# Small matrix products of two side lanes, written one at a time between large ones

## The chip, the cores and the metric

One core of one Trainium2 chip. The time is the device time of one execution in microseconds, the median of several runs; a profile is of one execution.

## What is computed

A decoder trunk of two layers on one sequence of 512 tokens with 1024 channels, all in float32. Cut to what matters here:

```python
for l in range(DEPTH):                       # 2
    h = rmsnorm(x, attn_norm[l])
    q_a, kv_a, g_a, q_b, k_b, v_b, uv_c = split(h @ w_in[l])
    o_a = nsa_attention(...)                 # 8 heads: compressed, selected and window branches, gated
    o_b = diff_attention(...)                # 4 heads, two softmax maps each, a = p0 - lam * p1
    o_c = chunked_sgu(uv_c, ...)             # per chunk of 128 tokens: lower-triangular product, times u
    gates = sigmoid(h @ w_merge[l] + b_merge[l])
    mixed = sum over branches of gates * (o @ w_branch)
    x = x + mixed @ w_out[l]
    h = rmsnorm(x, ffn_norm[l])
    x = x + (silu(h @ w_ffn1[l]) * (h @ w_ffn3[l])) @ w_ffn2[l]
return rmsnorm(x, final_norm)
```

## The kernel before

**The main stream.** Everything that multiplies by a weight matrix is a list of tasks (`layer_tasks`): the input projections, gates and branches (`merge_tasks`), the output projection, the feed-forward part. Weights come in chunks of 128 x 1024, are split into a high and a low half (ScalarE writes `wh` at L163, VectorE or GpSimd `wl` at L166), and each product of a 128 x 128 block is three matmuls of 512 columns: high x high, low x high, high x low (`mm3`, L184 to L186). `fm` and `tm` are generators around it; after three matmuls they yield 650, their rough length in ns. These 512-column matmuls are called large products here.

**The lanes.** Attention, the gating mixer and the softmax of the compressed branch are not tasks, but generators in two lanes (`aux_tasks`). Their TensorE work is small: transposes of 128 x 128 blocks of softmax weights (`sB` in `nsa`, L936; `sB` in `diff`, L1050), products of 128 columns (`sC` in `diff`, L1061; `prod` in `sgu_aux`, L764; `s0` in `cmp_soft`, L812), and logits of 128 to 512 columns (L878, L879). A lane's yield also states ns.

**What sets the order.** `run` goes through the tasks. Whenever the main stream yields c ns, each lane's balance grows by c (half of it in three slow tasks), and the lane is stepped until its balance is used up. So between two yields of the main stream, three large products, a lane writes all that it has between two of its own yields. `tick` counts main steps (for evacuations that are written so many steps later) and ns. A task that needs a lane's result steps the lanes until it is there. The tile framework then orders each engine's instructions by its own rules, with manual dependencies at a few places.

**Banks.** PSUM tiles come from four tags: three banks g (main stream), two banks s (logits, the mixer), two banks t (transposes and small products) and one bank o. A transposed block is read out of its bank t twice: ScalarE copies the high half (L937), VectorE subtracts for the low half (L945, written in `sL`). For the compressed softmax the same are L851 and L855.

Of the kernel before, what the change touches and what calls it, by code (L numbers as in the profile page):

```python
# [21 lines left out]
P, TT, KT, FT = 128, 4, 8, 22  # L22
# [9 lines left out]
D_MX, D_ACT, D_OA, D_XP = (2, 4), (7, 19), (3, 6, 17), 2  # L32
D_NORM = (10, 13)
W_NSA, W_DIFF, LAG = 470, 1200, 4
WARM = 14
SLOW = ("QA", "KB", "QB")
POOLED = {"g": 512}
# [43 lines left out]
class Kern:  # L81
# [35 lines left out]
        self.timed.append((self.clock + ns, key, fn))  # L117
        self.timed.sort(key=lambda e: e[0])

    def tick(self, ns=0):  # L120
        self.now += 1
        self.clock += ns
        while self.pending and self.pending[0][0] <= self.now:
            self.pending.pop(0)[2]()
        while self.timed and self.timed[0][0] <= self.clock:
            self.timed.pop(0)[2]()
# [52 lines left out]
    def mm3(self, out, w, x, k, kx, first, last, ts=slice(0, S)):  # L179
        nc = self.nc  # L180
        wh, wl = w
        xh, xl = x[kx] if isinstance(x[kx], tuple) else (x[kx][:, 0, :], x[kx][:, 1, :])
        c = slice(k * P, (k + 1) * P)
        nc.tensor.matmul(out, wh[:, c], xh[:, ts], start=first, stop=False)  # L184
        nc.tensor.matmul(out, wl[:, c], xh[:, ts], start=False, stop=False)  # L185
        nc.tensor.matmul(out, wh[:, c], xl[:, ts], start=False, stop=last)  # L186

    def fm(self, i0, evacs, x, K=KT, late=False, hooks=None, tag="g"):

        hooks = hooks or {}  # L190
        n = len(evacs)
        outs = [None] * n
        seq = [(m, k) for m in range(n) for k in range(K)]
        if late:
            cuts = late if isinstance(late, tuple) else (K - 1, K)
            seq = [(m, k) for a, b in zip((0,) + cuts, cuts) for m in range(n) for k in range(a, b)]
        for q, (m, k) in enumerate(seq):
            w = self.chunk(i0 + m)
            if outs[m] is None:
                outs[m] = self.bank(tag)  # L200
            self.mm3(outs[m], w, x, k, k, k == 0, k == K - 1)
            if (late and ((m == 0 and k == 5) or (m and k == K - 1))) or (not late and k == 3):
                self.ahead(i0 + m)
            if q in hooks:
                hooks[q]()
            if k == K - 1:
                evacs[m](outs[m])
            yield 650

    def tm(self, i0, x, evac, cuts, n, cs=None):  # L210

        nc = self.nc
        cs = range(len(cuts) - 1) if cs is None else cs
        if cs[0] == 0:
            self.tm_outs = [self.bank(b) for b in "gggo"]
        outs = self.tm_outs
        for c in cs:
            wh, wl = self.chunk(i0 + c - cs[0])
            for t in range(TT):
                ts = slice(t * P, (t + 1) * P)  # L220
                o = outs[t][:, :n]
                for k in range(cuts[c], cuts[c + 1]):
                    sl = slice((k - cuts[c]) * n, (k - cuts[c] + 1) * n)
                    nc.tensor.matmul(o, x[k][:, 0, ts], wh[:, sl], start=(k == 0), stop=False)  # L224
                    nc.tensor.matmul(o, x[k][:, 0, ts], wl[:, sl], start=False, stop=False)  # L225
                    nc.tensor.matmul(o, x[k][:, 1, ts], wh[:, sl], start=False, stop=(k == KT - 1))  # L226
                    yield 650 * n / 512
                if t == 0:
                    self.ahead(i0 + c - cs[0])
                if k == KT - 1:  # L230
                    evac(t, outs[t])
# [511 lines left out]
    def sgu_aux(self):  # L743
# [17 lines left out]
        def prod(t):  # L761
            ps = self.bank("s", [P, 4, P])
            for g in range(4):
                nc.tensor.matmul(ps[:, g, :], self.V[t][:, g * P:(g + 1) * P], wT[:, g, :],  # L764
                                 start=True, stop=True)
            return ps

        def mix(t, ps):
            tmp = self.t2("stmp", (P, 4, P))
# [17 lines left out]
        for t in range(TT + 2):  # L787
            if t + 1 < TT:
                norm(t + 1)
            if t < TT:  # L790
                pss[t] = prod(t)
                yield 1300
                tmps[t] = mix(t, pss.pop(t))
                yield 1300
            if t - 2 >= 0:
                split(t - 2, tmps.pop(t - 2))
                yield 650
# [3 lines left out]
    def cmp_soft(self, g, part):  # L801
# [5 lines left out]
        def s0():  # L807
            ps = st["ps"] = self.bank("t", [P, 4, P])
            for t in range(TT):
                ts = slice(t * P, (t + 1) * P)  # L810
                for ab in range(2):
                    nc.tensor.matmul(ps[:, t, :], raw[:, ab, ts],  # L812
                                     self.KAB[:, ab, g].rearrange("p h n -> p (h n)"),
                                     start=(ab == 0), stop=(ab == 1))
            st["e"] = e = self.t2("ce", (P, 4, 4, 32))
            st["ef"] = e.rearrange("p t h n -> p t (h n)")
            st["e3"] = e.rearrange("p t h n -> p (t h) n")
            nc.vector.tensor_tensor(st["ef"], ps, self.r4[:, :, None].to_broadcast([P, 4, P]), op=OP.mult)
# [27 lines left out]
        def s4():  # L846
            pt = st["pt"] = self.bank("t")
            for t in range(TT):
                nc.tensor.transpose(pt[:, t * P:(t + 1) * P], st["ef"][:, t, :], self.ident)
            pc = self.PcT[g] = self.t4("pcT", [P, 2, S], F32R)  # L850
            nc.scalar.activation(pc[:, 0, :], pt, AF.Copy)  # L851

# [1 line left out]
            pc = self.PcT[g]  # L854
            nc.vector.tensor_tensor(pc[:, 1, :], st["pt"], pc[:, 0, :].bitcast(F32), op=OP.subtract)  # L855

        for w, f in (((2600 * (g == 0), lambda: None), (1300, s0), (1300, s1), (1300, s2), (2600, ex)), ((2600, s3), (2600, s4), (1300, s5)))[part]:
            f()
            yield w

    def soft(self, s, n, i, sm=None):
# [20 lines left out]
    def nsa(self, g):  # L882
# [39 lines left out]
        def sB(v, part):  # L922
# [11 lines left out]
            for j in js:  # L934
                for h in range(2):
                    nc.tensor.transpose(pt[:, j - 2 * part, h, :], E[2 * v + h][:, j * P:(j + 1) * P], self.ident)  # L936
            nc.scalar.activation(hi, pt[:, 0:len(js)], AF.Copy)  # L937
            LO.append((lo, pt[:, 0:len(js)], hi))
            if js[-1] == i:
# [56 lines left out]
        for u in range(n + b + 3):  # L996
            if u == n:
                self.done.add("rows%d%d" % (g, l))
            if ok(u - 1):
                sN(u - 1)  # L1000
            if ok(u):
                sA(u)
            yield W_NSA
            w = u - b
            sL()
            if w % 2 and ok(w):
                sB(w // 2, 0)
            elif w % 2 == 0 and ok(w - 2):
                sB(w // 2 - 1, 1)
            if w % 2 == 0 and ok(w - 4):  # L1010
                sC(w // 2 - 2)
            yield W_NSA
        self.ensure("oa")


    def diff(self, p):
# [6 lines left out]
        def sA(u, j):  # L1023
            c, i = units[u]
            n = (i + 1) * P
            s = self.logits(q2[c][:, j], kh[c][:, j, :n], kl[c][:, j, :n], i)
            E[u, j] = self.soft(s, (i + 1) * P, i)

        def sN(u):
# [15 lines left out]
        def sB(u):  # L1045
            c, i = units[u]
            e = E.pop(u)
            pt = self.bank("t", [P, 4, P])
            for j in range(i + 1):
                nc.tensor.transpose(pt[:, j, :], e[:, j * P:(j + 1) * P], self.ident)  # L1050
            AT[u] = self.t2("at", (P, 4, P))
            nc.scalar.activation(AT[u][:, 0:i + 1, :], pt[:, 0:i + 1, :], AF.Copy)

        def sC(u):
# [5 lines left out]
            for j in range(i + 1):  # L1060
                nc.tensor.matmul(OB[c][:, i, :], at[:, j, :],  # L1061
                                 self.Vb[j // 2][:, j % 2, hd * P:(hd + 1) * P],
                                 start=(j == 0), stop=(j == i))
            if i == TT - 1:
                fin(c)

# [36 lines left out]
        for u in range(n + 4):  # L1103
            if ok(u - 1):
                sN(u - 1)
            if ok(u):
                sA(u, 0)
            yield W_DIFF
            if ok(u):
                sA(u, 1)  # L1110
            if ok(u - 2):
                sM(u - 2)
            yield W_DIFF
            if ok(u - 3):
                sB(u - 3)
            if ok(u - 4):
                sC(u - 4)
            yield W_DIFF
        if p == 1:
            yield from self.settle("ob", 600)  # L1120

# [94 lines left out]
    def ffn2(self, i0, m, evac):  # L1216
# [3 lines left out]
        for k in range(FT):  # L1220
# [2 lines left out]
            w = self.chunk(i0 + c)  # L1223
            if pos == 2:
                self.ahead(i0 + c)
            self.mm3(ps, w, self.act, pos, k, k == 0, k == FT - 1)
            if k == FT - 1:
                evac(ps)
            yield 650

# [23 lines left out]
    def ffn2_tail(self, i0):  # L1256
# [5 lines left out]
        m = KT - 1  # L1262
        for half in range(2):
            ts = slice(256 * half, 256 * half + 256)
            ps = self.bank("g")[:, :256]
            for k in range(FT):
                c, pos = divmod(m * FT + k, 8)
                w = self.chunk(i0 + c)
                if pos == 2 and half == 0:
                    self.ahead(i0 + c)  # L1270
                self.mm3(ps, w, self.act, pos, k, k == 0, k == FT - 1, ts)
                if k == FT - 1:
                    self.fin_evac(m, ts)(ps)
                if k == 12:
# [217 lines left out]
    def run(self):  # L1492
# [16 lines left out]
        def step(j):  # L1509
# [7 lines left out]
                c[1] = f()  # L1517
            try:
                w = next(c[1])
                self.tick(w if j else 0)  # L1520
                return w
            except StopIteration:
                self.done.add(lanes[j][c[0]][0])
# [5 lines left out]
        for n, chunks, f, need in tasks:  # L1529
# [4 lines left out]
                        raise RuntimeError("blocked: %s needs %s" % (n, x))  # L1534
            pace = (1, 0.5 if n[:2] in SLOW else 1)
            for c in f(i0):
                self.tick(c)
                for j in range(len(lanes)):
                    cur[j][2] += c * pace[j]
                    while cur[j][2] > 0:  # L1540
# [118 lines left out]
```

## Time and profile before

| | before |
|---|---|
| median of 3 runs | 1770.16 us (1769.95 to 1770.19) |
| the profiled execution | 1770.18 us, span 1768.3 us |
| TensorE busy | 1755.5 us, 99% of the span, 8436 matmuls |
| TensorE weight loads | 1465.0 us, 83% |
| VectorE / ScalarE / GpSimd busy | 968.9 / 751.4 / 354.0 us (55% / 42% / 20%) |
| granted TensorE clock | full (0.999) |

The span is the profiled part of the execution. Busy time of TensorE counts modelled ends: matmuls overlap in the records (one lasts 0.39 us and the next starts 0.23 us after it), so the time that a matmul costs is read from start to start. Weight loads are a separate row (PEld) and run beside matmuls.

### The profile page before, as it was taken

To read this page: it belongs to the slowest core of one execution; us is meant where nothing else is said; L and a number is where in the kernel's file an instruction comes from. 1 tells how busy PE (TensorE), PEld (TensorE's weight loads), DVE (VectorE), ACT (ScalarE), POOL (GpSimd) and SP (SyncE) were. 2 spreads that over 40 slices of the span, in tenths; PEclk is the share of its full clock that TensorE was granted. 3 is DMA by queue.
4 is the path that set the end of the run, shared out by engine and by line. 5 is a ranking of instruction groups with operands and counts; after the bars stand their busy time and mean duration, and the time that the engine had idled before them with its cause. 6 is when DMAs were issued, how large, how long until landed. Compare 5 with 4: busy or idle time off the path is not lost.

```text
span 1768.3 us, 22696 instructions
## 1 busy us (share of the span) xinstructions
PE 1755.5 (99%) x8436; PEld 1465.0 (83%) x8436; DVE 968.9 (55%) x1774; ACT 751.4 (42%) x1317; POOL 354.0 (20%) x355
## 2 busy tenths in 40 slices
PE   9999999999999999999999999999999999999998
PEld 7888888888888888888888888888888888888887
DVE  6877665665644444433366786746656444444223
ACT  6557663444333332222244576634533333322222
POOL 0244332444120000000012343214430200000000
PEclk9999999999999999999999999999999999999999
DMA  7571126532322222223344612255413232222221
GB/s 259 190 221 68 54 72 185 173 120 90 113 96 96 96 95 96 96 99 125 109 145 146 220 47 68 80 171 161 149 66 114 95 107 96 96 95 96 100 101 50
DMA packets 67726, 205.78 MB, mean 116 GB/s; under 512 B 8992, under 2 KB 9376, under 8 KB 67616
## 3 DMA queue, kind: packets, MB, share of 16 engines
q1 hardware_dynamic: 67472, 204.29, 34.6%
q8 instruction: 67, 1.10, 0.3%
q14 instruction: 43, 0.35, 0.1%
q10 hardware_dynamic: 144, 0.04, 0.0%
HBM read 185.29 MB, written 19.01 MB: 116 GB/s over the span
## 4 chain that ended last, share of the span: by engine, by line
PE 97%; DVE 1%; ACT 1%; DMA 0%; issue 0%; POOL 0%; SPq 0%; DVEq 0%; ACTq 0%; POOLq 0%
PE ps_g L184 26%; PE ps_g L185 26%; PE ps_g L186 26%; PE ps_o L958 2%; PE ps_t L936 2%; PE ps_s L879 2%; PE ps_g L224 2%; PE ps_s L878 2%; PE ps_g L225 2%; PE ps_g L226 2%; PE ps_o L1061 1%; DVE wl L166 1%; PE ps_o L226 1%; PE ps_o L224 1%; PE ps_o L225 0%; PE ps_t L1050 0%
## 5 line engine op out<-in xcount | busy, mean ns | idle before, releaser
L163 ACT ACTIVATE wh<-wr 128x1024 fp32r<-128x1024 f32 (+2 forms) x320 | 315.4, 989 | 654.2 <-PE ps_g L186 351.7
L184 PE MATMUL ps_g<-xg,wh 128*128 128x512 f32 x1400 | 553.8, 396 | 0.0
L185 PE MATMUL ps_g<-xg,wl 128*128 128x512 f32 x1400 | 546.8, 391 | 0.0
L186 PE MATMUL ps_g<-xg,wh 128*128 128x512 f32 x1400 | 546.2, 390 | 0.1
L166 DVE TENSOR_TENSOR wl<-wr,wh 128x1024 fp32r<-128x1024 f32 (+1 forms) x308 | 367.5, 1195 | 234.8 <-ACT wh L163 231.3
L186 PEld LDWEIGHTS ps_g<-xg,wh 128*128 128x128 f32 x1400 | 262.8, 188 | 56.2 <-DVE xg L283 1.0
L184 PEld LDWEIGHTS ps_g<-xg,wh 128*128 128x128 f32 x1400 | 263.2, 188 | 50.4 <-ACT xg L280 0.5
L185 PEld LDWEIGHTS ps_g<-xg,wl 128*128 128x128 f32 x1400 | 263.3, 188 | 49.0 <-DVE wl L290 0.3
L869 ACT ACTIVATE e<-e,nm 128x384 f32<-128x384 f32 (+2 forms) x192 | 107.2, 559 | 89.0 <-DVE nm L867 85.0
L184 PE MATMUL ps_g<-act,wh 128*128 128x512 f32 (+1 forms) x374 | 141.2, 378 | 0.0
L185 PE MATMUL ps_g<-act,wl 128*128 128x512 f32 (+1 forms) x374 | 140.8, 376 | 0.0
L186 PE MATMUL ps_g<-act,wh 128*128 128x512 f32 (+1 forms) x374 | 140.8, 376 | 0.0
L497 POOL TENSOR_TENSOR acc<-acc,sq 128x512 f32<-128x512 f32 x18 | 29.3, 1626 | 433.6 <-ACT sq L496 433.6
L919 POOL TENSOR_SCALAR e<-e,sm,ga 128x128 f32<-128x128 f32 (+3 forms) x128 | 82.1, 652 | 111.8 <-DVE sm L915 88.7
L867 DVE CUSTOM_DVE_ANT_0 e<-ps_s,con 128x384 f32<-128x384 f32 (+2 forms) x192 | 90.8, 483 | 22.3 <-PE ps_s L879 20.7
L1202 DVE TENSOR_TENSOR fb<-ps_g,R 128x512 f32<-128x512 f32 x44 | 30.4, 691 | 129.1 <-PE ps_g L186 129.1
L166 POOL TENSOR_TENSOR wl<-wr,wh 128x512 fp32r<-128x512 f32 x48 | 72.6, 1513 | 117.7 <-ACT wh L163 117.7
L1193 DVE TENSOR_TENSOR fa<-ps_g,R 128x512 f32<-128x512 f32 x44 | 30.4, 691 | 95.7 <-PE ps_g L186 95.7
L186 PEld LDWEIGHTS ps_g<-act,wh 128*128 128x128 f32 x374 | 70.3, 188 | 13.0
L184 PEld LDWEIGHTS ps_g<-act,wh 128*128 128x128 f32 x374 | 70.3, 188 | 12.9
L185 PEld LDWEIGHTS ps_g<-act,wl 128*128 128x128 f32 x374 | 70.4, 188 | 12.8
L945 DVE TENSOR_TENSOR pt<-ps_t,pt 128x512 fp32r<-128x512 f32 (+1 forms) x96 | 56.7, 597 | 27.4 <-ACT pt L937 27.2
(248 smaller groups left out, 2474.2 us busy)
## 6 DMA issues: line engine op xcount, KB each, us to landing
wr<-in_wst SPq DMA_DIRECT2D x266, 512.0 KB, 3.3
rp_d<-pc SPq DMA_DIRECT2D x112, 128.0 KB, 3.6
wr<-in_wst SPq DMA_DIRECT2D x52, 256.0 KB, 2.6
q<-rp_d SPq DMA_DIRECT2D x16, 512.0 KB, 5.9
kh<-rp_d SPq DMA_DIRECT2D x24, 256.0 KB, 5.8
xT<-in_xT SPq DMA_DIRECT2D x7, 512.0 KB, 6.2
kl<-rp_d SPq DMA_DIRECT2D x12, 256.0 KB, 6.8
xtok<-in_xtok SPq DMA_DIRECT2D x4, 512.0 KB, 8.7
```

Source lines behind the costliest of these rows:

```text
L163: nc.scalar.activation(h[:, :w], t[:, :w], AF.Copy)
L166: eng.tensor_tensor(lo[:, a:b], t[:, a:b], h[:, a:b].bitcast(F32), op=OP.subtract)
L184: nc.tensor.matmul(out, wh[:, c], xh[:, ts], start=first, stop=False)
L185: nc.tensor.matmul(out, wl[:, c], xh[:, ts], start=False, stop=False)
L186: nc.tensor.matmul(out, wh[:, c], xl[:, ts], start=False, stop=last)
L224: nc.tensor.matmul(o, x[k][:, 0, ts], wh[:, sl], start=(k == 0), stop=False)
L225: nc.tensor.matmul(o, x[k][:, 0, ts], wl[:, sl], start=False, stop=False)
L226: nc.tensor.matmul(o, x[k][:, 1, ts], wh[:, sl], start=False, stop=(k == KT - 1))
L867: nc.vector.tensor_tensor_reduce(out=e[:, :n], in0=s[:, :n], in1=self.mask[:, S - n:], scale=-0.125, scalar=3e38, op0=OP.add, op1=OP.min, ...
L869: nc.scalar.activation(e[:, :n], e[:, :n], AF.Exp, bias=nm, scale=-1.0, accum_out=sm)
L919: nc.gpsimd.tensor_scalar(e[:, :n], e[:, :n], sm[:, h:h + 1], self.ga[:, i, b:b + 1], op0=OP.mult, op1=OP.mult)
L945: nc.vector.tensor_tensor(lo, pt, hi.bitcast(F32), op=OP.subtract)
```

## The change

Every matmul of the main stream and most small ones of the lanes get a yield of their own. A yield that is a tuple is a part of a step: it adds ns and lets the lanes run, but does not count as a step for evacuations that are written later. The main stream now yields 650 / 3 ns after each of the three matmuls, and a lane yields the same after each transpose or small product; the lanes' other yields are made shorter, so that a step's sum stays about as it was.

```diff
+BIG = 650 / 3
...
-    def tick(self, ns=0):
-        self.now += 1
+    def tick(self, ns=0, step=1):
+
+        self.now += step
...
         nc.tensor.matmul(out, wh[:, c], xh[:, ts], start=first, stop=False)
+        yield BIG,
         nc.tensor.matmul(out, wl[:, c], xh[:, ts], start=False, stop=False)
+        yield BIG,
         nc.tensor.matmul(out, wh[:, c], xl[:, ts], start=False, stop=last)
...
-            self.mm3(outs[m], w, x, k, k, k == 0, k == K - 1)
+            yield from self.mm3(outs[m], w, x, k, k, k == 0, k == K - 1)
...
-            yield 650
+            yield BIG
...
                 nc.tensor.matmul(ps[:, g, :], self.V[t][:, g * P:(g + 1) * P], wT[:, g, :],
                                  start=True, stop=True)
-            return ps
+                yield BIG,
+            pss[t] = ps
...
-                pss[t] = prod(t)
-                yield 1300
+                yield from prod(t)
+                yield 450
...
-        for w, f in (((2600 * (g == 0), lambda: None), (1300, s0), (1300, s1), (1300, s2), (2600, ex)), ((2600, s3), (2600, s4), (1300, s5)))[part]:
-            f()
+        for w, f in (((2600 * (g == 0), lambda: None), (450, s0), (1300, s1), (1300, s2), (2600, ex)), ((2600, s3), (1750, s4), (1300, s5)))[part]:
+            parts = f()
+            if parts is not None:
+                yield from parts
...
                     nc.tensor.transpose(pt[:, j - 2 * part, h, :], E[2 * v + h][:, j * P:(j + 1) * P], self.ident)
+                    yield BIG,
...
-            yield W_NSA
+            yield W_NSA * 0.6
...
-                sB(w // 2, 0)
+                yield from sB(w // 2, 0)
             elif w % 2 == 0 and ok(w - 2):
-                sB(w // 2 - 1, 1)
+                yield from sB(w // 2 - 1, 1)
...
-            yield W_NSA
+            yield W_NSA / 4
...
                 nc.tensor.transpose(pt[:, j, :], e[:, j * P:(j + 1) * P], self.ident)
+                yield BIG,
...
-            yield W_DIFF
+            yield W_DIFF * 0.75
...
             if ok(u - 3):
-                sB(u - 3)
+                yield from sB(u - 3)
             if ok(u - 4):
-                sC(u - 4)
-            yield W_DIFF
+                yield from sC(u - 4)
+            yield W_DIFF * 0.5
...
                 w = next(c[1])
-                self.tick(w if j else 0)
+                part = isinstance(w, tuple)
+                w = w[0] if part else w
+                self.tick(w if j else 0, not part)
...
             for c in f(i0):
-                self.tick(c)
+                part = isinstance(c, tuple)
+                c = c[0] if part else c
+                self.tick(c, not part)
```

`tm`, `ffn2` and the products of `sC` in `diff` are treated the same way; the last quarter of the last projection (`ffn2_tail`) keeps its steps.

TensorE's queue in layer 0, where the gating mixer starts (`prod`, L764 before and L770 after, into `ps_s`; L184 to L186 before are L186, L188 and L190 after), before:

```order
L764 MATMUL ps_s<-sw,v 128x128 x4
L184 MATMUL ps_g<-xg,wh 128x512
L185 MATMUL ps_g<-xg,wl 128x512
L186 MATMUL ps_g<-xg,wh 128x512
L184 MATMUL ps_g<-xg,wh 128x512
```

and now:

```order
L770 MATMUL ps_s<-sw,v 128x128
L188 MATMUL ps_g<-xg,wl 128x512
L770 MATMUL ps_s<-sw,v 128x128
L190 MATMUL ps_g<-xg,wh 128x512
L770 MATMUL ps_s<-sw,v 128x128
L186 MATMUL ps_g<-xg,wh 128x512
L770 MATMUL ps_s<-sw,v 128x128
L188 MATMUL ps_g<-xg,wl 128x512
```

Four products of one chunk, one clump before, have one large product between each two now.

TensorE's queue in the head of the first attention lane of layer 0 (L936 before and L947 after are transposes into `ps_t`, L878/L879 and L889/L890 logits, L958/L970 and L969/L981 products with the values), before:

```order
L936 MATMUL ps_t<-con,e 128x128 x2
L184 MATMUL ps_g<-oc,wh 128x512
L936 MATMUL ps_t<-con,e 128x128 x4
L185 MATMUL ps_g<-oc,wl 128x512
L186 MATMUL ps_g<-oc,wh 128x512
L936 MATMUL ps_t<-con,e 128x128 x4
L878 MATMUL ps_s<-kh,q_1217 128x384
L879 MATMUL ps_s<-kl,q_1217 128x384
L184 MATMUL ps_g<-xg,wh 128x512
```

and now:

```order
L947 MATMUL ps_t<-con,e 128x128 x8
L889 MATMUL ps_s<-kh,q_1213 128x512
L970 MATMUL ps_o<-pt,v_1129 128x512
L890 MATMUL ps_s<-kl,q_1213 128x512
L889 MATMUL ps_s<-kh,q_1213 128x512
L890 MATMUL ps_s<-kl,q_1213 128x512
L970 MATMUL ps_o<-pt,v_1129 128x512
L970 MATMUL ps_o<-pt,v_1129 128x2x128 x2
L947 MATMUL ps_t<-con,e 128x128 x6
L970 MATMUL ps_o<-pt,v_1129 128x512 x2
L970 MATMUL ps_o<-pt,v_1129 128x2x128 x2
L981 MATMUL ps_o<-pcT,VCS 128x256 x4
```

Here the lane's products have moved together: these 30 products have no large product of the main stream between them. The same stands in layer 1.

## Rows read from the trace of the kernel before

**Rows 1.** The page: busy us of each engine, its share of the span, its instructions.
```profile
PE 1755.5 (99%) x8436; PEld 1465.0 (83%) x8436; DVE 968.9 (55%) x1774; ACT 751.4 (42%) x1317; POOL 354.0 (20%) x355
```

**Rows 2.** Waits of PE: line, what ended it; us, times, longest.
```profile
PE ps_g L224 <- DVE raw L679: 2.5, 2, 1.9
...
PE ps_t L936 <- DVE pcT L855: 0.9, 2, 0.4
PE ps_s L764 <- DVE stmp L770: 0.6, 1, 0.6
```

**Rows 3.** Timeline of PE, large products alone: start us, us, instruction.
```profile
600.08 0.39 PE L186 MATMUL ps_g<-xg,wh 128*128 128x512 f32 x1
...
611.19 0.39 PE L184 MATMUL ps_g<-xg,wh 128*128 128x512 f32 x1
```

**Rows 4.** Timeline of PE around a clump of four transposes.
```profile
441.30 0.60 PE L1090 MATMUL ps_t<-con,do 128*128 128x128 f32 x4
441.66 0.48 PE L184 MATMUL ps_g<-xg,wh 128*128 128x512 f32 x1
441.97 0.40 PE L185 MATMUL ps_g<-xg,wl 128*128 128x512 f32 x1
...
444.51 0.39 PE L184 MATMUL ps_g<-xg,wh 128*128 128x512 f32 x1
```

**Rows 5.** Timeline of PE around a clump of eight fp32 records.
```profile
1245.65 1.05 PE L1061 MATMUL ps_o<-vb,at 128*128 128x128 f32 x8
...
1247.92 0.22 PE L878 MATMUL ps_s<-kh,q 128*128 128x128 f32 x1
```

**Rows 6.** Timeline of PE around a transpose that stands alone.
```profile
332.89 0.28 PE L1050 MATMUL ps_t<-con,e 128*128 128x128 f32 x1
332.92 0.48 PE L184 MATMUL ps_g<-xg,wh 128*128 128x512 f32 x1
333.24 0.40 PE L185 MATMUL ps_g<-xg,wl 128*128 128x512 f32 x1
...
333.70 0.22 PE L878 MATMUL ps_s<-kh,q 128*128 128x128 f32 x1
```

**Rows 7.** Timeline of PE around another lone transpose.
```profile
1206.29 0.27 PE L1050 MATMUL ps_t<-con,e 128*128 128x128 f32 x1
...
1206.63 0.39 PE L185 MATMUL ps_g<-xg,wl 128*128 128x512 f32 x1
```

**Rows 8.** Timeline of PEld, the weight loads around the transpose of rows 6.
```profile
332.66 0.14 PEld L1050 LDWEIGHTS ps_t<-con,e 128*128 128x128 f32 x1
332.89 0.19 PEld L184 LDWEIGHTS ps_g<-xg,wh 128*128 128x128 f32 x1
333.01 0.19 PEld L185 LDWEIGHTS ps_g<-xg,wl 128*128 128x128 f32 x1
```

**Rows 9.** Timelines of PE, ACT and DVE in the head of attention, layer 0.
```profile
143.85 0.58 ACT L851 ACTIVATE pcT<-ps_t 128x512 fp32r<-128x512 f32 x1
144.46 0.69 DVE L855 TENSOR_TENSOR pcT<-ps_t,pcT 128x512 fp32r<-128x512 f32 x1
145.29 0.41 PE L936 MATMUL ps_t<-con,e 128*128 128x128 f32 x2
146.25 0.42 DVE L945 TENSOR_TENSOR pt<-ps_t,pt 128x256 fp32r<-128x256 f32 x1
146.37 0.72 ACT L869 ACTIVATE e<-e,nm 128x512 f32<-128x512 f32 x1 [0.24 <-DVE nm L867]
146.45 0.40 PE L186 MATMUL ps_g<-oc,wh 128*128 128x512 f32 x1
146.82 0.63 PE L936 MATMUL ps_t<-con,e 128*128 128x128 f32 x4
```

**Rows 10.** Timeline of PE, products of 256 columns in a row.
```profile
83.71 0.28 PE L595 MATMUL ps_s<-wl,xh 128*128 128x256 f32 x1
...
84.42 0.28 PE L595 MATMUL ps_s<-wl,xh 128*128 128x256 f32 x1
```

More of the change, by code (lines that the diff above doesn't have):

```diff
@@ L224, in tm @@
                     nc.tensor.matmul(o, x[k][:, 0, ts], wh[:, sl], start=(k == 0), stop=False)
+                    yield BIG * n / 512,
                     nc.tensor.matmul(o, x[k][:, 0, ts], wl[:, sl], start=False, stop=False)
+                    yield BIG * n / 512,
                     nc.tensor.matmul(o, x[k][:, 1, ts], wh[:, sl], start=False, stop=(k == KT - 1))
-                    yield 650 * n / 512
+                    yield BIG * n / 512
                 if t == 0:
@@ L936, in sB @@
                     nc.tensor.transpose(pt[:, j - 2 * part, h, :], E[2 * v + h][:, j * P:(j + 1) * P], self.ident)
+                    yield BIG,
             nc.scalar.activation(hi, pt[:, 0:len(js)], AF.Copy)
@@ L1025, in sA @@
             n = (i + 1) * P
-            s = self.logits(q2[c][:, j], kh[c][:, j, :n], kl[c][:, j, :n], i)
+            ts = slice(i * P, n)
+            s = self.bank("s")
+            nc.tensor.matmul(s[:, :n], q2[c][:, j, ts], kh[c][:, j, :n], start=True, stop=False)
+            if i == 0:
+                yield BIG,
+            nc.tensor.matmul(s[:, :n], q2[c][:, j, ts], kl[c][:, j, :n], start=False, stop=True)
             E[u, j] = self.soft(s, (i + 1) * P, i)
@@ L1050, in sB @@
                 nc.tensor.transpose(pt[:, j, :], e[:, j * P:(j + 1) * P], self.ident)
+                yield BIG,
             AT[u] = self.t2("at", (P, 4, P))
@@ L1063, in sC @@
                                  start=(j == 0), stop=(j == i))
+                yield BIG,
             if i == TT - 1:
@@ L1106, in diff @@
             if ok(u):
-                sA(u, 0)
-            yield W_DIFF
+                yield from sA(u, 0)
+            yield W_DIFF * 0.75
             if ok(u):
-                sA(u, 1)
+                yield from sA(u, 1)
             if ok(u - 2):
                 sM(u - 2)
-            yield W_DIFF
+            yield W_DIFF * 0.75
             if ok(u - 3):
-                sB(u - 3)
+                yield from sB(u - 3)
             if ok(u - 4):
-                sC(u - 4)
-            yield W_DIFF
+                yield from sC(u - 4)
+            yield W_DIFF * 0.5
         if p == 1:
@@ L1225, in ffn2 @@
                 self.ahead(i0 + c)
-            self.mm3(ps, w, self.act, pos, k, k == 0, k == FT - 1)
+            yield from self.mm3(ps, w, self.act, pos, k, k == 0, k == FT - 1)
             if k == FT - 1:
                 evac(ps)
-            yield 650
+            yield BIG
     def fin_x(self, k, ts=slice(0, S)):
@@ L1270, in ffn2_tail @@
                     self.ahead(i0 + c)
-                self.mm3(ps, w, self.act, pos, k, k == 0, k == FT - 1, ts)
+                for _ in self.mm3(ps, w, self.act, pos, k, k == 0, k == FT - 1, ts):
+                    pass
                 if k == FT - 1:
```

## The prediction

> **What bounds the kernel now.** I read the page first. TensorE is busy 1755.5 us, 99% of the span, while VectorE has 55% and ScalarE 42% [rows 1]; the granted clock of the execution is the full one, the upper of its two levels, so that no clock is to be won. So the sum of what TensorE's instructions cost is the time, and another engine counts only where TensorE visibly waits for it. The list of waits has little: 2.5 us at the V projection, 0.9 us for a transpose bank, 0.6 us for a bank of the gating mixer [rows 2]. These waits understate a little, because a matmul's end is modelled longer than the pace (390 ns against 227 ns below) and hides a short gap. I therefore take prices from starts, not from durations.
>
> **Prices, from starts to starts.** A stream of 512-column products: 49 steps from 600.08 to 611.19 us [rows 3], so 0.2267 us each; weight loads are hidden in it. Small products come in several surroundings:
> - A clump of four transposes begins at 441.30; 12 large products follow before the start at 444.51 [rows 4]. 3.21 - 12 x 0.2267 = 0.49 us. The clump with the first large product alone ends at 441.97: 0.67 - 0.227 = 0.44, which is 0.111 us per transpose. The other 0.05 us is a tail: the next large products come some ns late, until the pace is regained.
> - Eight records of an fp32 product (four products, two records each) take from 1245.65 with six large products to 1247.92 [rows 5]: 2.27 - 1.36 = 0.91 us, 0.114 us each with tail.
> - A transpose that already stands alone: 332.89 to 333.70 with three large products [rows 6], 0.81 - 0.68 = 0.13 us; with the next large product only (to 333.24), 0.35 - 0.227 = 0.123 us. Another, 1206.29 to 1206.63 [rows 7], gives 0.113 us. A lone start followed by one at 0.03 us is the recorder's way of showing this pair; only the sum of both counts.
>
> Why a small product costs 0.11 us everywhere is seen in the load rows: the transpose's load starts with the large product before it (332.66), the next large product's load starts only with the transpose itself (332.89), and the load after that 0.12 us later [rows 8]. One load runs ahead, not two. A load that stands beside a large product is free, a load beside a small product is the price; and each small product, wherever it stands, has exactly one load beside it.
>
> **The change, part by part.** No product, evacuation or transfer is added or removed: 8256 products in both orders, of them 688 below 256 columns (868 records, since 180 products are recorded twice). What changes is where they stand. I counted in the built orders: 189 clumps become 534, of which 476 are single products; 334 of the 533 distances between clumps are one product (before: 6). "Tails", clumps with at least five other products behind them, go from 165 to 144.
> - The base, 868 records x 0.111 us = 96 us, is the same in both.
> - Each additional start of a clump costs what a single has over 0.111: 0.002 [rows 7] to 0.012 us [rows 6]. I take the middle, 0.007: 345 x 0.007 = +2.4 us. The bounds are +0.7 and +4.1.
> - Tails: 0.49 - 4 x 0.111 = 0.046, less the 0.007 already counted, so about 0.04 us [rows 4]; 21 fewer save 0.8 us. Bounds: nothing, and the same 0.8.
> - Yields that give a lane another pace: two steps of the attention lane make 940 before; now 282 + 118 + on average 2.5 transposes x 217 = 942. A step of differential attention makes 3600 before, and 2400 + about 5.5 x 217 = 3590 now. The first step of the compressed softmax grows from 1300 to 450 + 8 x 217 = 2183, which moves its consumers four large products later. All of it lies beside TensorE's large products, so I cost it at nothing; if the cover fails, it shows as a wait at V, whose price today is 2.5 us [rows 2].
> - In the other lanes' queues (ScalarE, VectorE, GpSimd) only the order of neighbours changes, and DMA issues hardly move. With these engines at 55% or less [rows 1] I take nothing, and leave the waits to the rivals.
>
> Sum: +2.4 - 0.8 = +1.6 us. The profiled execution took 1770.18 us (span 1768.3 and 1.9 around it), and the median of the runs is 1770.16, so the sum stands for both: **1771.8 us**. About 0.2%, 3.5 us, is what a measurement of this kernel can tell from no change: below 1766.6 it is faster, above 1773.7 slower. The forecast's own range, with the bounds above, is 1770.1 to 1774.3; if every new start paid a full isolated single, 0.13 - 0.111, it would be +6.6 and 1776.8.
>
> One page of the Trainium skill, "TensorE: Matmul & The Clock Gate", section "Back-to-back issue gap", gives about 81 ns per product of 128 columns in a sustained stream of loads and products. By that figure 476 singles would each save 30 ns and the sum would be -14 us (an estimate from that page). The trace does not agree: 111 ns in clumps and 113 to 123 ns alone [rows 4, 6, 7].
>
> **Rivals.**
> *No more than the load (forecast), 47%.* As above; not distinguishable from no change.
>
> *A transpose bank comes late, 35% with the high end of the forecast's starts: slower.* There are two banks of tag t. A fill waits until ScalarE has copied the fill two before it (0.58 us) and VectorE has subtracted (0.69 us). Where the first attention lane of a layer catches up, this is already tight: VectorE's row L855 ends at 145.15 and the transposes start at 145.29; L945 ends at 146.67 and four transposes start at 146.82, and there the large product before them takes 0.37 instead of 0.227 us [rows 9]. That is a wait of 0.14 us today. In the new order this same place, in both layers, has 30 lane products without one large product: eight transposes (two fills) in a row and six more behind eight attention products. Before, large products lay between. A fill lasts 0.44 us and its release 1.27 us, so the fill after next lacks up to 0.8 us, and with an exponential of 0.72 us (L869) ahead on ScalarE and another 0.69 us step ahead on VectorE up to 2.2. One such wait in each layer: +1.6 to +4.4 us, 1773.4 to 1776.2. A spread fill also holds its bank longer everywhere: 4 x 0.111 + 3 x 0.227 = 1.1 instead of 0.44 us. It decides from +1.9 us on. For it: the tight rows. Against it: the rest of the trace has hardly any wait for this tag, 0.9 us in total [rows 2].
>
> *The load is hidden, 8%: faster.* If a single between large products needed only its own columns, it would take 0.2267 - 384 x slope; the slope is from 256-column products, six steps from 83.71 to 84.42 [rows 10], 0.118 each: (0.2267 - 0.118) / 256 = 0.42 ns a column, so 0.066 us. Saving 0.045 us on 476 singles gives -21 us, 1750. It needs two loads ahead of the running product; rows 8 show one. The same would follow from the change's idea, that a small load hides behind a large product: it does, but the large product's load then stands bare instead.
>
> *Waits go away, 10%: faster or same.* If a smoother order removed the 2.5, 0.9 and 0.6 us [rows 2], it would be 1771.8 - 4.0 = 1767.8, still within 0.2%; only with the low end of the starts (+0.7 - 0.8) does it reach 1766.1. The wait at V hangs on VectorE and ScalarE work whose order hardly moves there, so I do not expect it to go.
>
> **How the numbers follow.** Same 0.47: the forecast, less its high end, with part of the vanishing waits. Slower 0.35: banks that come late, or starts that cost 0.012 us and more. Faster 0.18: hidden loads 0.08, and waits that vanish together with cheap starts or in places that I have not seen, 0.10. The likeliest time is 1771.8. The range leaves the 8% of hidden loads out below; it reaches down to 1764, where all the waits named are gone and starts are free with a little over, and up to 1780, where the bank waits (+4.4) come on top of the high starts (+4.1): 1778.7, and a little over for spread fills elsewhere.
>
> **What would show it.** Right: TensorE's share stays at 99%; a lone transpose and the large product behind it take 0.34 to 0.35 us together; dense stretches of alternating products show no third price; the list of waits has the same names with under 8 us. Wrong on the slower side: waits of transposes (ps_t) for VectorE's copies of the low half in the head of each layer's first attention lane, or large products at 0.37 us and more ahead of them. Wrong on the faster side: a lone transpose with its large product in under 0.30 us. The prediction fails as a whole if records of large products in dense stretches step by more than 0.24 us, a price that the trace of before cannot show, since it has only six distances of one product.

## The result and the profile after

| | before | after |
|---|---|---|
| median | 1770.06 us (1769.92 to 1770.19, 4 runs) | 1787.03 us (1786.92 to 1787.11, 4 runs) |
| the profiled execution's span | 1768.3 us | 1785.2 us |

The ratio is 1.0092, 95% interval [1.0079, 1.0104]: the change costs 17 us, where +1.6 was forecast, and lies outside the range. The page of the changed kernel, in the columns of [rows 1]:

```profile
PE 1764.1 (99%) x8436; PEld 1460.0 (82%) x8436; DVE 978.5 (55%) x1774; ACT 746.5 (42%) x1317; POOL 349.3 (20%) x355
```

The same instructions, the same 99%: the share of the engine that is always busy says nothing here, because modelled ends of matmuls fill short gaps. The list of waits of PE, in the columns of [rows 2], does:

```profile
PE ps_s L889 <- DVE nm L878: 5.0, 4, 2.2
PE ps_t L947 <- DVE pt L957: 2.8, 7, 1.1
PE ps_s L1040 <- DVE nm L878: 2.7, 4, 1.0
...
PE ps_s L770 <- DVE stmp L777: 1.0, 2, 0.6
...
PE ps_g L228 <- DVE raw L685: 0.2, 1, 0.2
```

The first and third names were not in [rows 2]: the logits of the first attention lane (L889) and of differential attention (L1040) wait for a bank s, until VectorE has added the mask (L878). Transposes wait 2.8 us in place of 0.9, now for the low half of their own blocks (L957, `sL`). The V projection (L228, L224 before) waits 0.2 in place of 2.5.

The price of singles is not the cause. A dense stretch of single transposes in PE's timeline of the changed kernel (start us, us, instruction):

```profile
176.30 0.27 PE L947 MATMUL ps_t<-con,e 128*128 128x128 f32 x1
176.32 0.48 PE L188 MATMUL ps_g<-xg,wl 128*128 128x512 f32 x1
176.64 0.27 PE L947 MATMUL ps_t<-con,e 128*128 128x128 f32 x1
176.67 0.48 PE L190 MATMUL ps_g<-xg,wh 128*128 128x512 f32 x1
176.99 0.27 PE L947 MATMUL ps_t<-con,e 128*128 128x128 f32 x1
```

From 176.30 to 176.99 two pairs take 0.69 us; less two large products of 0.2267 [rows 3] that is 0.118 us for a transpose. The two singles of before took 0.123 and 0.113 [rows 6, 7]. The Trainium skill's page "TensorE: Matmul & The Clock Gate", section "Back-to-back issue gap", has about 81 ns for such a product; this stretch does not agree either.

Where the time goes is seen by lining up both traces by the number of the main stream's product. At the end of the V projection of layer 0 the changed kernel is 1.2 us ahead, and at that of layer 1 it gains another 0.5. It loses 3.9 us beside the first attention lane of layer 0, 3.5 beside differential attention, 7.8 and 3.5 in layer 1: 18.7 - 1.7 = 17.0, within rounding the 16.9 at the end. In the long stretches without an attention lane the distance stays the same within 0.01 us. The same product behind the lanes of layer 0, before and now, and another behind those of layer 1 (6.18 and 16.93 us later):

```profile
449.95 0.39 PE L184 MATMUL ps_g<-xg,wh 128*128 128x512 f32 x1
456.13 0.39 PE L186 MATMUL ps_g<-xg,wh 128*128 128x512 f32 x1
...
1458.98 0.39 PE L185 MATMUL ps_g<-xg,wl 128*128 128x512 f32 x1
1475.91 0.39 PE L188 MATMUL ps_g<-xg,wl 128*128 128x512 f32 x1
```

The longest wait stands at the start of the first attention lane of layer 1. PE's and DVE's timeline there (in brackets the idle time before and what ended it):

```profile
1008.71 2.17 DVE L658 TENSOR_SCALAR VCS<-vcs,con 128x256 fp32r<-128x256 f32 x4
...
1009.15 0.28 PE L889 MATMUL ps_s<-kh,q 128*128 128x256 f32 x1
...
1009.61 0.28 PE L889 MATMUL ps_s<-kh,q 128*128 128x256 f32 x1
...
1010.81 0.67 DVE L845 TENSOR_REDUCE csm<-ce 128x16 f32<-128x512 f32 x1
1011.01 0.39 PE L190 MATMUL ps_g<-xg,wh 128*128 128x512 f32 x1
...
1012.11 0.28 DVE L878 CUSTOM_DVE_ANT_0 e<-ps_s,con 128x128 f32<-128x128 f32 x1
...
1013.13 0.28 DVE L878 CUSTOM_DVE_ANT_0 e<-ps_s,con 128x128 f32<-128x128 f32 x1
1013.34 0.28 DVE L878 CUSTOM_DVE_ANT_0 e<-ps_s,con 128x128 f32<-128x128 f32 x1
...
1013.57 0.67 PE L889 MATMUL ps_s<-kh,q 128*128 128x512 f32 x1 [2.17 <-DVE nm L878]
...
1014.47 0.63 PE L186 MATMUL ps_g<-xg,wh 128*128 128x512 f32 x1
1014.89 0.63 PE L188 MATMUL ps_g<-xg,wl 128*128 128x512 f32 x1
```

The lane's first two logits fill both banks s at 1009.15 and 1009.61, each with two blocks, so that four masks read them. The third logits come in PE's queue only six large products after the second and are due at 1011.24. VectorE is still at other work (L658, L845) and starts the first of the four masks at 1012.11 and the last at 1013.34; the first bank is read by the first and the third (1013.13). TensorE waits for that, 2.17 us in all, and the next large product, which stands behind these logits in its queue, starts at 1014.47. Layer 0 has the same wait, 2.07 us before 133.41, and all of the 5.0 us at L889 is found at the third logits of a first attention lane. In layer 1 more follows, as the windows show (start and end, length, busy time of PE, PEld, DVE, ACT, POOL with the number of instructions, then the granted clock, the DMA engines' share and GB/s):

```profile
1011.00:1013.00 2.00, 0.40 (x2) 0.00 (x0) 1.90 (x8) 0.49 (x2) 0.00 (x0) 1.00 0.90 260
1013.00:1014.00 1.00, 0.43 (x1) 0.41 (x2) 0.64 (x7) 0.75 (x4) 0.00 (x0) 0.84 0.81 283
1014.00:1015.00 1.00, 1.00 (x4) 0.76 (x3) 0.29 (x1) 0.51 (x4) 0.00 (x0) 0.50 0.86 340
...
1016.00:1017.00 1.00, 1.00 (x4) 0.70 (x4) 0.59 (x4) 0.06 (x1) 0.21 (x1) 0.50 0.03 10
1017.00:1018.00 1.00, 1.00 (x8) 0.75 (x7) 0.74 (x5) 1.00 (x5) 0.98 (x3) 0.96 0.00 0
```

After the wait the granted clock is 0.50, the lower level, for about 3 us; products of 512 columns step by 0.43 us in place of 0.227, about 1.4 us in all.

### The profile page after: what moved, and what is told of

Read it like the earlier page. It is cut to its first block, busy times and chain, and to the rows that moved or that the text cites. A ratio compares the mean times of both kernels' runs of the same rounds, so it can differ in the third digit from the quotient of the medians.

```text
span 1785.2 us, 22688 instructions
## 1 busy us (share of the span) xinstructions
PE 1764.1 (99%) x8436; PEld 1460.0 (82%) x8436; DVE 978.5 (55%) x1774; ACT 746.5 (42%) x1317; POOL 349.3 (20%) x355
## 4 chain that ended last, share of the span: by engine, by line
PE 91%; DVE 4%; ACT 2%; issue 1%; POOL 1%; DMA 1%; SPq 0%; DVEq 0%; ACTq 0%; POOLq 0%
PE ps_g L186 25%; PE ps_g L188 25%; PE ps_g L190 25%; PE ps_o L970 2%; PE ps_t L947 2%; PE ps_g L228 1%; PE ps_g L230 1%; PE ps_g L232 1%; PE ps_o L1079 1%; PE ps_s L889 1%; PE ps_s L890 1%; DVE wl L168 1%; ACT wh L165 1%; PE ps_t L1067 0%; PE ps_o L232 0%
## 5 line engine op out<-in xcount | busy, mean ns | idle before, releaser
L186 PE MATMUL ps_g<-xg,wh 128*128 128x512 f32 x1400 | 559.7, 400 | 0.4 <-ACT xg L286 0.2
L188 PE MATMUL ps_g<-xg,wl 128*128 128x512 f32 x1400 | 556.7, 398 | 0.0
L190 PE MATMUL ps_g<-xg,wh 128*128 128x512 f32 x1400 | 556.0, 397 | 0.1
L168 DVE TENSOR_TENSOR wl<-wr,wh 128x1024 fp32r<-128x1024 f32 (+1 forms) x308 | 359.4, 1169 | 234.3 <-ACT wh L165 233.8
L186 PEld LDWEIGHTS ps_g<-xg,wh 128*128 128x128 f32 x1400 | 263.7, 188 | 55.1 <-ACT wh L165 0.9
L190 PEld LDWEIGHTS ps_g<-xg,wh 128*128 128x128 f32 x1400 | 263.4, 188 | 54.3 <-DVE xg L289 0.8
L188 PEld LDWEIGHTS ps_g<-xg,wl 128*128 128x128 f32 x1400 | 263.6, 188 | 53.0 <-DVE wl L296 0.3
L186 PE MATMUL ps_g<-act,wh 128*128 128x512 f32 (+1 forms) x374 | 141.2, 378 | 0.0
L188 PE MATMUL ps_g<-act,wl 128*128 128x512 f32 (+1 forms) x374 | 140.8, 376 | 0.0
L190 PE MATMUL ps_g<-act,wh 128*128 128x512 f32 (+1 forms) x374 | 140.8, 376 | 0.0
L930 POOL TENSOR_SCALAR e<-e,sm,ga 128x128 f32<-128x128 f32 (+3 forms) x128 | 78.2, 621 | 133.8 <-DVE sm L926 108.5
L878 DVE CUSTOM_DVE_ANT_0 e<-ps_s,con 128x384 f32<-128x384 f32 (+2 forms) x192 | 90.4, 482 | 21.7 <-PE ps_s L890 10.9
L947 PE MATMUL ps_t<-con,e 128*128 128x128 f32 x320 | 82.0, 274 | 3.0 <-DVE pt L957 2.8
L190 PEld LDWEIGHTS ps_g<-act,wh 128*128 128x128 f32 x374 | 70.4, 188 | 13.0
L188 PEld LDWEIGHTS ps_g<-act,wl 128*128 128x128 f32 x374 | 70.4, 188 | 12.8
L186 PEld LDWEIGHTS ps_g<-act,wh 128*128 128x128 f32 x374 | 70.4, 188 | 12.8
```

The source lines that it names most:

```text
L168: eng.tensor_tensor(lo[:, a:b], t[:, a:b], h[:, a:b].bitcast(F32), op=OP.subtract)
L878: nc.vector.tensor_tensor_reduce(out=e[:, :n], in0=s[:, :n], in1=self.mask[:, S - n:], scale=-0.125, scalar=3e38, op0=OP.add, op1=OP.min, ...
L930: nc.gpsimd.tensor_scalar(e[:, :n], e[:, :n], sm[:, h:h + 1], self.ga[:, i, b:b + 1], op0=OP.mult, op1=OP.mult)
```

## The experiments

Two theories stood against each other. **Pace**: the lanes' other yields were shortened by a fixed part, but the yields that replace them come only where a small product is written. A step of the first attention lane without one is 282 + 118 = 400 long, before 940; one of differential attention 2400, before 3600. There the lane writes logits faster than VectorE empties two banks (it alone reads them; ScalarE works on the masked copy `e`). **Spread**: the singles themselves hold banks longer and put other engines' work in a worse order.

**E1, singles at the pace of before.** The change, but each step's yields are what was there before, less 217 per small product c that it writes:

```diff
-            yield W_NSA * 0.6
+            rest = 2 * W_NSA - BIG * c
+            yield rest / 2
...
-            yield W_NSA / 4
+            yield rest / 2
```

and in `diff` three yields of `(3 * W_DIFF - BIG * c) / 3`. Expected: 

> Singles as in the change, but each step of the two attention lanes lasts as long as before the change: the step's length less 217 for each small product in it, shared over its plain yields (940 in the selected/window attention, 3600 in the differential one). Theory pace (steps without transposes had shrunk from 940 to 400 and from 3600 to 2400, so logits come faster than VectorE and ScalarE empty the two banks s): the waits for VectorE's row maxima go, and the time is 1769 to 1775. Rival spread (a small product that stands alone keeps banks and the order of the other engines worse, whatever the pace): at least 1783.

Measured: 1770.87 us (1770.45 to 1771.28, 10 runs), before on the same chip 1771.21; ratio 1.000 [0.9991, 1.001]. The waits for banks s are gone. The same place in E1's PE timeline:

```profile
1002.93 0.28 PE L889 MATMUL ps_s<-kh,q 128*128 128x256 f32 x1
...
1004.09 0.28 PE L889 MATMUL ps_s<-kh,q 128*128 128x256 f32 x1
...
1008.51 0.39 PE L889 MATMUL ps_s<-kh,q 128*128 128x512 f32 x1
```

The third logits come 5.6 us after the first, not 2.1, and find their bank free, although VectorE's long step L658 takes 2.18 us here too.

**E2, clumps at the pace of the change.** No yields between the small products of the attention lanes; each step as long as under the change (`yield W_NSA / 4 + BIG * c`). Expected: 

> The converse: in the two attention lanes the small products stand in clumps again, with no yield between them, but each step is as long as in the change (short where it has no transposes, long where it has four). The main stream keeps its yield after each large product. Theory pace: the waits of the change come back without singles, 1781 to 1789. Rival spread: 1769 to 1774.

Measured: 1783.51 us (1782.11 to 1784.5, 4 runs), ratio 1.0072 [1.0057, 1.0087]. Its waits of PE:

```profile
PE ps_s L889 <- DVE nm L878: 5.0, 4, 2.2
PE ps_s L1043 <- DVE nm L878: 2.7, 4, 1.0
PE ps_t L947 <- DVE pt L956: 2.1, 3, 1.5
```

These are to the tenth the waits for banks s of the changed kernel, with the transposes of these lanes in clumps. Spread falls as the main cause. The changed kernel is 3.5 us slower still; singles cost 1.5 us of that at the pace of before (E1 against E3, below), and E2's profiled execution has no fall of the clock.

**E3, clumps at the pace of before.** In the attention lanes everything as before; the main stream's yields, the mixer and the compressed softmax as changed. Expected: 

> Clumps and the pace of before in the two attention lanes; of the change only the main stream's yield after each large product stays, and the singles of the gating mixer and of the compressed softmax. Both theories: 1767 to 1773. If it is near the change (1780 and more), both are wrong and the cause is the main stream's finer yield or the other two lanes.

Measured: 1769.33 us (1768.83 to 1769.84, 10 runs), ratio 0.9993 [0.9983, 1.0003].

**E4, only the short steps lengthened.** The change, with

```diff
-            yield W_NSA / 4
+            yield W_NSA / 4 if c else W_NSA * 1.4
...
-            yield W_DIFF * 0.5
+            yield W_DIFF * 0.5 if c else W_DIFF * 1.5
```

Expected: 

> As the change, but steps of the attention lanes that have no small product at all get before's length (940 and 3600); all other steps stay uneven (834 to 1267, and more). Theory pace, with the lanes' heads as the main place: 1774 to 1780, and no wait at the first logits of a lane. If unevenness inside the lane weighs as much as its head: 1780 to 1785. Rival spread: at least 1783.

Measured: 1774.72 us (1774.38 to 1775.93, 10 runs), ratio 1.0023 [1.0014, 1.0033]. About 12 of the 17 us go with the length of the steps that have no small product. (With them the whole first attention lane is 41,020 long, more than the 36,660 of before.) Waits that are left:

```profile
PE ps_t L947 <- DVE pt L957: 1.6, 4, 0.5
PE ps_s L1044 <- DVE nm L878: 1.4, 2, 0.7
```

**E5, only the short steps, in the kernel before.** Clumps, the main stream's coarse yields, and the change's length for steps without a small product alone:

```diff
-            yield W_NSA
+            yield W_NSA if c else W_NSA * 0.6
...
-            yield W_NSA
+            yield W_NSA if c else W_NSA / 4
```

and likewise in `diff`. Expected: 

> The kernel before (clumps, yields of the main stream after three large products), with one thing of the change: the steps of the two attention lanes in which no small product is written have the change's length (400 in place of 940, 2400 in place of 3600); steps with small products stay at 940 and 3600. If short steps in the lanes' heads are the main cause, the waits of logits for VectorE (L878 here, 5.0 us in the changed kernel) come back without any single product, and the time is 1777 to 1785 us. If it takes singles beside them, it stays at 1769 to 1773.

Measured: 1784.15 us (1782.22 to 1785.61, 5 runs), ratio 1.0074 [1.0061, 1.0087]. The short steps alone bring the loss back. Two falls of the clock in its profiled execution of 1785.6 us (at 117 and 1254 us) are not the whole of it: two runs took 1782.2 and 1782.5, with a higher mean clock (0.998 and 0.999 against 0.997). The size can't be compared with the change's, since here the first attention lane is 28,550 long, shorter than under the change (32,930). The waits are shared out otherwise than expected, as many at transposes as at logits:

```profile
PE ps_t L936 <- DVE pt L945: 3.1, 4, 1.3
PE ps_s L878 <- DVE nm L867: 3.0, 8, 0.7
PE ps_g L224 <- DVE raw L679: 2.4, 2, 1.9
```

**E6, only the longer first step of the compressed softmax.** In the kernel before, `(1300, s0)` is made `(2183, s0)`, to see whether this took the wait from the V projection. Expected: 

> The kernel before with one number changed: the first step of the compressed softmax has 2183 in place of 1300, its length under the change. If this step alone removes the wait at the V projection (2.5 us before, 0.2 in the changed kernel), the time is 1767.3 to 1768.6 us. If the wait went for another reason (the main stream's finer yields, or the singles), it stays at 1770 to 1771.

Measured: 1772.92 us (1771.72 to 1773.31, 11 runs), ratio 1.0009 [1.0001, 1.0018]: a miss, above both ranges. The wait stays at 2.5 us. Lined up with the kernel before, the profiled execution loses 1.5 us right behind this wait, by a fall of the clock (end of this document), and another 0.7 and 0.8 us beside the first attention lanes of the two layers: the longer step costs there too.

**E7, the pace of the first attention lane alone put back.** The change with E1's yields in `nsa` only. Expected: 

> The change, with the length of before (940, less 217 per small product) for the steps of the first attention lane alone; differential attention keeps the change's lengths. By the shifts of the large products in the changed kernel, the first lane's stretches gave 3.9 + 7.8 us and the differential ones 3.5 + 3.5 us. If the two lanes act each for itself, this kernel takes 1775 to 1779 us; if the differential lane is only late because the first one is, it takes 1769 to 1773.

Measured: 1774.88 us (1774.55 to 1775.17, 11 runs), ratio 1.0021 [1.0012, 1.0031], just under "each for itself". Lined up with the kernel before, its differential attention loses 2.1 and 2.0 us, not the 3.5 and 3.5 of the changed kernel: the lanes do not act wholly each for itself. Of its waits:

```profile
PE ps_s L1045 <- DVE nm L878: 1.8, 4, 0.6
...
PE ps_t L947 <- DVE pt L957: 0.2, 1, 0.2
```

The transposes' waits are all but gone with the first lane's old pace.

**E8 and E9, where the wait at V went.** E8 is the kernel before with the main stream's fine yields alone; E9 adds the compressed softmax's products one at a time, with the change's steps. Expected of E8: 

> The kernel before with the main stream's yields alone made fine (one after each large product); every lane has its clumps and its step lengths of before. The lengthened first step of the compressed softmax did not remove the wait at the V projection (2.5 us stayed). If the main stream's finer yields remove it, the V projection waits 0.2 us and the time is 1767.5 to 1769.5 us. If the single products of the mixer or of the compressed softmax do, the wait stays at 2.5 and the time at 1769.5 to 1772.

Expected of E9: 

> As the kernel with fine yields of the main stream alone, and the products of the compressed softmax written one at a time with the change's step lengths; the mixer and both attention lanes as before. If the compressed softmax's spreading removes the wait at the V projection, it is 0.2 us here and the time 1767.5 to 1769.5; if only the mixer's singles do, the wait stays and the time is 1769.5 to 1772.

Measured: E8 1771.14 us (1769.26 to 1771.81, 11 runs), ratio 1.0001 [0.9992, 1.001]; E9 1769.12 us (1768.77 to 1769.81, 11 runs), 0.9993 [0.9984, 1.0001]. The row of the V projection in E8's list of waits, then in E9's:

```profile
PE ps_g L228 <- DVE raw L685: 2.8, 2, 1.9
```

```profile
PE ps_g L228 <- DVE raw L685: 0.2, 1, 0.2
```

So the wait goes away with the compressed softmax's products written one at a time, together with their steps; the length of the first step alone (E6) does not take it. E9 and E3 have the lowest medians of all, but their intervals reach to no change: no version is shown to beat the kernel before.

## Why the prediction was wrong

**The step that failed** is "Yields that give a lane another pace", costed at nothing. The runs put about 16 us in its place (E1 with the old pace 1770.87, the changed kernel 1787.03). It has two errors. The first is the arithmetic: the steps were compared by an average ("on average 2.5 transposes", "about 5.5" products), taken over the units of work (80 / 32 and 44 / 8), while the lanes have more steps than units. Counted from the code, a first attention lane has 39 steps and 80 transposes, 2.05 a step; its sum is 39 x 400 + 80 x 217 = 32,930, before 36,660. A differential lane has 12 steps and 44 such yields: 38,330, before 43,200. The lanes are 10 to 11% shorter as a whole, where the text on the change has "about as it was". The second is that an average was used where the order matters. Transposes lag the logits by four units (`LAG`), so the first five steps of a first attention lane have none: 2000 now, 4700 before. The first four of a differential lane sum to 10,250 in place of 14,400. It is there that little but logits is written, and that banks run out: the 5.0 us at L889 and 2.0 of the 2.7 us at L1040 are waits of a lane's fifth unit, right behind its first four steps, and the other 0.7 stands in the second step of a differential lane. That the second error weighs more is read from these places; no run keeps the short steps and restores the lane's sum, or the other way round.

**The cover.** "All of it lies beside TensorE's large products" holds as long as a lane's product finds its bank free. In the trace above TensorE starts its products in the order of its queue: logits that stand too early stop the large products behind them as well (1014.47). That VectorE is busy 55% of the span [rows 1] told nothing of the 4.8 us from 1008.71 to 1013.55, in which it works nearly without a gap.

**What held.** The sum for singles, +1.6 us, in its size: E1 and E3 have the same pace, E1 has 379 more single products, and on one chip they lie 1.5 us apart, without a run in common (from 1770.45, up to 1769.84). The mean price, 0.118 in the stretch above, is inside the bounds of [rows 6, 7].

**The rival of the late transpose bank** named waits of `ps_t` for VectorE's low half, +1.6 to +4.4 us; 2.8 us were listed. But its place was wrong, and that the size fits is luck: at the head of [rows 9] nothing is listed, the waits stand at 188.75 and 254.88 and, in layer 1, between 1053 and 1139 us. The 30 products in a row are in the changed kernel's trace (147.39 to 152.02 us), without a listed wait. E7, with the first lane's old pace, has no such row, and 0.2 us of these waits.

**The wait at V** was to grow if the cover failed. It shrank from 2.5 to 0.2 us, as a rival had it ("waits go away"); this gain of 1.7 us (1.2 and 0.5 in the lined-up traces) was swamped.

**The balance.** Each step adds one thing, from medians: before 1770.06; fine main stream, mixer and compressed softmax (E3) 1769.33; singles in the attention lanes (E1) +1.5; the change's pace in differential attention (E7) +4.0; in the first attention lane (after) +12.2: 1787.03. E7 and the changed kernel ran on other chips than E1 and E3. On the chip of E1 and E3 the kernel before has 1771.21, since 13 of its 25 runs have a lower mean clock (end of this document); against the other 12, with a median of 1769.86, E3 is 0.5 faster and E1 1.0 slower, which its ratio of 1.000 hides. Of the last step, +12.2, about 3 us arise in differential attention: there the changed kernel loses 7.0 us, E7 4.1. The listed new waits, 5.0 + 2.7 + 2.8 - 0.9 = 9.6 us, and the low clock, 1.4, leave some 5 of the 16 us of pace. Gaps that matmuls' modelled ends hide can be about half of that (a wait is listed 0.39 - 0.227 = 0.16 us too short, and there are 15); the rest is not itemised here.

**What would have shown it** was in reach: the order of TensorE's queue at the lanes' heads, counting large products between the second and the third logits, and VectorE's rows at that place.

## What to carry to other kernels

When yields or weights that set a pace are redistributed, check the sum of each step in order, the first steps above all, not the mean over a lane: a side stream that comes early costs as much as its banks' release, because an in-order engine stops for it with everything behind. To separate a new granularity from a new pace, run the new granularity with the old sums (E1) and the old granularity with the new ones (E2). An engine's 99% cannot tell waits from work; the list of waits, and starts lined up with the trace of before, can.

## What was not expected of the hardware

A wait of about 2 us is sometimes followed by the lower clock, and sometimes not. Before the V projection of layer 0 TensorE stands for 1.94 us in the kernel before, and the clock stays at 1.00 from 114 to 126 us. E6 and E8 have the same wait there (1.93 and 1.94 us). The windows behind it, first of the kernel before, then E6's, then E8's:

```profile
116.00:118.00 2.00, 1.46 (x11) 1.46 (x12) 1.75 (x3) 1.11 (x1) 2.00 (x2) 1.00 0.97 347
118.00:120.00 2.00, 2.00 (x16) 1.78 (x15) 0.07 (x1) 1.99 (x5) 1.85 (x2) 1.00 0.71 217
```

```profile
116.00:118.00 2.00, 1.39 (x6) 1.40 (x7) 2.00 (x3) 0.00 (x0) 2.00 (x2) 0.69 0.96 350
118.00:120.00 2.00, 2.00 (x11) 2.00 (x10) 0.33 (x2) 1.39 (x2) 1.77 (x2) 0.50 0.73 232
```

```profile
118.00:120.00 2.00, 2.00 (x10) 2.00 (x10) 0.42 (x1) 1.99 (x3) 1.94 (x2) 0.50 0.44 136
120.00:122.00 2.00, 2.00 (x11) 1.81 (x10) 0.00 (x0) 1.25 (x3) 0.57 (x1) 0.65 0.97 342
```

E6's products of the main stream are 1.5 us later behind this place than in the kernel before. The changed kernel shows the same: nearly equal waits of 2.07 us (layer 0, clock 1.00 in every window up to 138 us) and 2.17 us (layer 1, clock 0.50). A page of the Trainium skill ("TensorE: Matmul & The Clock Gate", "What's actually happening") says that the chip watches activity in a window that runs freely, not in step with the kernel; that equal waits ended differently agrees with it, but no run here shows the window. E5's second fall stands right behind two shorter waits, of 0.70 and 0.75 us, that end at 1251.62 and 1253.33.

The runs of the kernel before fall into two groups by their mean granted clock, without an exception on three chips: 37 runs with 0.999 took 1769.54 to 1770.92 us, 30 runs with 0.998 took 1771.21 to 1772.18. A fall costs about as much as lies between the groups, 1.5 us. E3 and E9, without the wait at V, spread over 1 us alone (1768.77 to 1769.84). That the falls of the kernel before come behind its wait at V is not shown, since its profiled execution has none, and the wait is not the whole of the spread: E6 keeps it and spreads over 1.6 us, E4 lacks it and spreads over 1.55. If they do, a short wait costs not only itself, but now and then 1.5 us more.
